# Fetching the routed rows of three expert pairs by indirect transfers instead of one-hot products

## The chip, the core and the metric

One core of a Trainium2 chip runs the whole program. Its engines work side by side, each through its own list of instructions in order: PE (TensorE, matrix products and transposes), DVE (VectorE), ACT (ScalarE), POOL (GpSimd) and SP (SyncE), which here issues nearly all DMA transfers. The transfers themselves are carried by 16 DMA engines. An instruction starts when its engine is free and the semaphores that it waits for are set. The metric is the time on the device of one execution in microseconds (us), lower is better.

## The reference

Two blocks run one after the other on 512 tokens of width 1024. The change lies in the first block's expert layer, `expert_choice`. Each of the 16 experts picks its 64 best tokens (cap = 2 * 512 / 16), takes their rows, runs a gated network of width 1024 on them and adds the weighted result back:

```python
def expert_choice(h, w_router, w_gate, w_up, w_down):
    b, l, _ = h.shape
    cap = CAP_FACTOR * l // N_EXPERTS
    aff = jax.nn.softmax(jnp.einsum('bld,de->ble', h, w_router).astype(jnp.float32), axis=-1)
    vals, idx = lax.top_k(jnp.swapaxes(aff, 1, 2), cap)
    bidx = jnp.arange(b)[:, None, None]
    xs = h[bidx, idx]
    hid = jax.nn.silu(jnp.einsum('becd,edf->becf', xs, w_gate)) * jnp.einsum('becd,edf->becf', xs, w_up)
    y = jnp.einsum('becf,efd->becd', hid, w_down) * vals[..., None].astype(h.dtype)
    return jnp.zeros_like(h).at[bidx, idx].add(y)
...
        hx2 = modulate(rmsnorm(x, g_norm2[l]), sh2, sc2)
        x = x + ga2 * expert_choice(hx2, w_router[l], w_gate_e[l], w_up_e[l], w_down_e[l])
```

`rmsnorm` scales a token's row by a factor of its own, and `modulate` scales and shifts it column by column. What is fetched in the kernel is the row times its factor; the columns' scale and shift are applied after the transpose, where the columns lie on the partitions.

## The kernel before

Before the stage (`phase_a2`) the residual `xres` is finished token tile by token tile (four tiles of 128 tokens). `ev_x` adds the branch's output and sums the squares on ACT, and `row_rstd` turns the sums into the tile's factor `rs[t]`. `logits` transposes all tokens, multiplies by the router and takes the softmax. A loop of eight rounds on DVE then finds the 64 best tokens of every expert. The result is `idxF`, 128 x 8: column p holds the token numbers of pair p, 64 of expert 2p above 64 of expert 2p+1. Beside this chain PE works on a projection of the second block's memory (`mem_k`, `mem_v`, lines 89 to 91 on the tiles `wH`, `wL`, `mH`, `mL`).

The stage itself (`phase_b`) runs over eight pairs of experts. For one pair:

- `gather(p)` brings the 128 rows to PE, transposed: `rows_b` spreads the pair's token numbers over the partitions with a product (tile `bcI`, L1060) and compares them with the token numbers on DVE (`G`, 4 tiles of 128 x 128, L1063). `G` is one-hot in the tokens and carries their factor. Then 8 column blocks x 4 token tiles = 32 products `xres` by `G` (L1101) give `xT`.
- `pair_mm` (L1090) multiplies by the gate and the up matrix, each 2 x 1024 x 1024. `hidden` multiplies both results and transposes them (L1128).
- `pair_mm` on the down matrix and `scatter` (L1141 to L1152): ACT and POOL split the weighted result into two parts (`yH`, L1146, and `yL`, L1147), PE puts them at their tokens' places (`mm2`, L96 and L97), and DVE adds. Pair 7 has `last_down` (L1118), whose two halves of the output come one after the other, and a tile `gg` in between.

In an instruction listing a product of 64 rows is one of two that share PE, and a listed fp32 product is two instructions in the trace.

Weights come in chunks of 1 MB, 8 for a gate, up or down matrix of a pair, 24 a pair. Each is one transfer issued by SP in the program's order (`raw`, L118) into a tile `raw` of 8 KB a partition. `raw_tile` gives the tiles in turn from four pools of 16 buffers in all: a list of pools is walked round and round, and within a pool its buffers follow one another. Asking for a tile outside this walk (`gg`, `self.rawp.tile`) moves the turn of the pool `rawp` alone. A transfer waits until what lay in its buffer was read, and SP, which issues in order, stands still meanwhile, with all transfers behind it.

A scheduler orders the instructions of each engine from the program's order and its model of durations; the listings below show the result.

## Time and profile before

| | us |
|---|---|
| median of 3 runs | 1707.64 (1706.93 to 1708.19) |
| profiled execution | 1707.27 |
| span of its trace | 1705.5 |
| PE busy | 1574.8 (92%) |
| DVE busy | 855.0 (50%) |
| ACT busy | 613.2 (36%) |
| POOL busy | 565.1 (33%) |

The first expert stage lies at about 533 to 1015 us of the span. Windows show what each engine did in such a stretch, a timeline gives single instructions in order of time, and the waits tell who stood still and for whom. A row of a timeline that covers several instructions has their number behind an x, and its length is that of all together. In brackets stands how long the engine was idle before it, and what ended that. The times of SP's rows are those of issuing a transfer, and a transfer lands later.

### The profile page before, as it was taken

Reading aid. Unit: us, or ns where it says so; the run is one execution under the profiler, and the core shown is the slowest. Engines: PE = TensorE matmul, PEld = TensorE weight load, DVE = VectorE, ACT = ScalarE, POOL = GpSimd, SP = SyncE. Lnnn points to the kernel's source line nnn. Section 1 sums busy time; section 2 is a strip of 40 time slices with the busy share of each in tenths; the row PEclk is TensorE's granted clock in tenths of the full one; section 3 lists DMA queues with packets and bytes.
Section 4 is the critical chain, followed back from the end, with each engine's and each line's share of the span. In section 5 each row is a group of like instructions: output and inputs, shape, how many; then the busy total and the mean of one; then the engine's idle time right before and its main releaser. Section 6 shows DMA issues by size and latency. Waiting matters only on the chain. (4 is left out here: it accounts for less than half of the span.)

```text
span 1705.5 us, 20869 instructions
## 1 busy us (share of the span) xinstructions
PE 1574.8 (92%) x7702; PEld 1044.6 (61%) x7702; DVE 855.0 (50%) x1595; ACT 613.2 (36%) x1277; POOL 565.1 (33%) x447
## 2 busy tenths in 40 slices
PE   5988899999999999999999979999999989789994
PEld 3766667777776444344344337778676766566663
DVE  4388554423554122022102137997754473667776
ACT  3443364433432000000000034325763354467773
POOL 1223324344523000000000014576443342657765
PEclk9989999999999999999999989999999999889997
DMA  8522413354746999999999983232112328369944
GB/s 290 187 98 89 134 56 111 129 183 155 273 163 256 397 408 409 409 409 409 409 409 408 408 266 128 88 99 75 51 49 87 124 86 322 111 244 344 343 162 166
DMA packets 165548, 381.23 MB, mean 224 GB/s; under 512 B 16302, under 2 KB 74742, under 8 KB 165436
## 3 DMA queue, kind: packets, MB, share of 16 engines
q1 hardware_dynamic: 161116, 371.63, 58.9%
q0 software_dynamic: 4320, 8.16, 1.3%
q8 instruction: 63, 1.03, 0.2%
q14 instruction: 49, 0.40, 0.1%
HBM read 367.40 MB, written 19.93 MB: 227 GB/s over the span
## 5 line engine op out<-in xcount | busy, mean ns | idle before, releaser
L130 POOL TENSOR_TENSOR wL<-raw,wH 128x512 fp32r<-128x512 f32 x220 | 312.5, 1426 | 420.7 <-ACT wH L129 394.8
L1090 PE MATMUL ps<-raw,xT 128*64 128x512 f32 x1024 | 240.8, 595 | 0.0
L129 ACT ACTIVATE wH<-raw 128x512 fp32r<-128x512 f32 x240 | 149.6, 628 | 253.1 <-PE ps L90 145.6
L1090 PEld LDWEIGHTS ps<-raw,xT 128*64 128x64 f32 x1024 | 74.3, 137 | 137.3 <-issue 133.4
L1147 POOL TENSOR_TENSOR yL<-y,yH 128x512 fp32r<-128x512 f32 x14 | 17.9, 1279 | 419.4 <-ACT yH L1146 409.2
L1144 DVE SCALAR_TENSOR_TENSOR y<-ps,valF,ga 128x512 f32<-128x512 f32 x16 | 12.0, 751 | 226.2 <-PE ps L1090 206.8
L91 PE MATMUL ps<-raw,wL 128*128 128x512 f32 (+1 forms) x320 | 120.6, 377 | 3.0 <-POOL wL L130 3.0
L89 PE MATMUL ps<-raw,wH 128*128 128x512 f32 (+1 forms) x320 | 121.4, 379 | 0.7 <-ACT raw L188 0.7
L90 PE MATMUL ps<-raw,wH 128*128 128x512 f32 (+1 forms) x320 | 121.0, 378 | 0.0
L1338 DVE SCALAR_TENSOR_TENSOR cacc<-upad,dwc,cacc 128x512 f32<-128x512 f32 x120 | 117.8, 1035 | 0.9
L1090 PE MATMUL ps<-raw,hidT 128*64 128x512 f32 x448 | 109.2, 594 | 2.9 <-DMA raw<-in_w_down_e 2.9
L89 PE MATMUL ps<-hx,wH 128*128 128x512 f32 x224 | 92.3, 412 | 2.0 <-ACT wH L129 2.0
L91 PE MATMUL ps<-hx,wL 128*128 128x512 f32 x224 | 90.1, 402 | 1.2 <-POOL wL L130 1.2
L1904 DVE TENSOR_TENSOR wL<-raw,wH 128x512 fp32r<-128x512 f32 x96 | 88.5, 976 | 4.7 <-ACT wH L1903 3.4
L1924 POOL TENSOR_TENSOR dL<-raw,dH 128x512 fp32r<-128x512 f32 x64 | 81.7, 1295 | 27.8 <-ACT dH L1923 27.3
L90 PE MATMUL ps<-hx,wH 128*128 128x512 f32 x224 | 90.8, 405 | 0.0
L1146 ACT ACTIVATE yH<-y 128x512 fp32r<-128x512 f32 x16 | 10.0, 626 | 212.4 <-DVE y L1144 212.4
L1129 ACT ACTIVATE hidT<-pa 128x512 f32<-128x512 f32 x16 | 9.6, 597 | 205.0 <-PE pa L1128 205.0
L1090 PEld LDWEIGHTS ps<-raw,hidT 128*64 128x64 f32 x448 | 36.2, 137 | 73.5 <-issue 62.9
L91 PEld LDWEIGHTS ps<-raw,wL 128*128 128x128 f32 x320 | 61.1, 191 | 15.0 <-POOL wL L130 3.4
L89 PEld LDWEIGHTS ps<-raw,wH 128*128 128x128 f32 x320 | 61.3, 192 | 12.3 <-ACT raw L188 1.1
L90 PEld LDWEIGHTS ps<-raw,wH 128*128 128x128 f32 x320 | 61.1, 191 | 11.5 <-issue 0.5
(618 smaller groups left out, 3401.6 us busy)
## 6 DMA issues: line engine op xcount, KB each, us to landing
raw<-in_w_gate_e SPq DMA_DIRECT2D x64, 1024.0 KB
raw<-in_w_up_e SPq DMA_DIRECT2D x64, 1024.0 KB
raw<-in_w_down_e SPq DMA_DIRECT2D x64, 1024.0 KB
raw<-in_w_in SPq DMA_DIRECT2D x34, 1024.0 KB
raw<-in_w_ada SPq DMA_DIRECT2D x24, 1024.0 KB
raw<-in_expert_w_gate SPq DMA_DIRECT2D x32, 512.0 KB
raw<-in_expert_w_up SPq DMA_DIRECT2D x32, 512.0 KB
raw<-in_expert_w_down SPq DMA_DIRECT2D x16, 1024.0 KB
```

Source lines behind the costliest of these rows:

```text
L89: mm(ps, l[0], r[0], start=first, stop=False)
L90: mm(ps, l[0], r[1], start=False, stop=False)
L91: mm(ps, l[1], r[0], start=False, stop=last)
L129: i = self.nc.scalar.activation(out=H, in_=raw_ap, func=AF.Copy)
L130: j = (eng or self.lsub).tensor_tensor(out=L, in0=raw_ap, in1=H, op=OP.subtract)
L1090: nc.tensor.matmul(ps[o, :], act[:, k, o], r[:, q, h * 512:(h + 1) * 512], start=k == 0, stop=k == 7, tile_position=(0, 64 * i))
L1144: V.scalar_tensor_tensor(y, py[e], self.valF[:, p:p + 1], ga2[:, e, :], op0=OP.mult, op1=OP.mult)
L1146: AC.activation(out=H, in_=y, func=AF.Copy)
L1147: (nc.gpsimd if p < 7 else V).tensor_tensor(out=L, in0=y, in1=H, op=OP.subtract)
L1338: V.scalar_tensor_tensor(acc, src, c, acc, op0=OP.mult, op1=OP.add)
L1904: V.tensor_tensor(out=L3, in0=w, in1=H3, op=OP.subtract)
L1924: (nc.gpsimd, V)[DL[i]].tensor_tensor(out=L, in0=src, in1=H, op=OP.subtract)
```

## The change

After `rs[t]` is known, ACT writes the token tile times its factor into two tiles `xn` and SP writes them to `xnd`, a table of 512 rows of 4 KB in device memory. The token numbers are also kept as integers (`idxU`). For the pairs 3, 5 and 7 `gather` no longer builds `G`: POOL issues an indirect transfer that fetches the 128 rows named by a column of `idxU` into a tile of the ring of weight buffers, and PE transposes them in 8 blocks. The other five pairs are gathered as before. `idxF` and `valF` move to another pool.

```diff
--- before.py
+++ after.py
@@ -31,6 +31,7 @@
 NRAW_B2 = 3
 NRAW_B3 = 6
 NRAW_B4 = 1
+ROWS_D = 3, 5, 7
 NRAW_D = 4
 NGA = 24
 NY = 3
@@ -887,6 +888,7 @@
             V.tensor_tensor(sel, sel, ident[:, q:q + 16], op=OP.add)
         nc.sync.dma_start(out=wr, in_=I["w_router"][0].rearrange("(k p) c -> p k c", p=128))
         self.rs4 = cst.tile([128, 4], F32, name="rs4")
+        self.xnd = self.drp.tile([512, 1024], F32, name="xnd")
         self.tokid = cst.tile([128, 4], F32, name="tokid")
         nc.sync.dma_start(out=self.tokid, in_=I["tokid"])
         affT = self.pa(256, name="affT")
@@ -987,6 +989,11 @@
                 self.mm3(ps, (mS2[0][k][:, tk], mS2[1][k][:, tk]), wS[k], k == 0, k == 7)
             ev_x(t, 1, ps)
             rs[t] = self.row_rstd(sm, sss[t], out=self.rs4[:, t:t + 1])
+            for e in range(2):
+                c = slice(e * 512, (e + 1) * 512)
+                xn = tc_(name="xn")
+                AC.activation(out=xn, in_=xres[:, t, c], func=AF.Copy, scale=rs[t])
+                nc.sync.dma_start(out=self.xnd[tk, c], in_=xn)
         logits()
         late.close()
         rows = self.pool(right, "rows", 1, "right")
@@ -1030,11 +1037,13 @@
         V.tensor_tensor(bidx, two[:, 1, 0:16], two[:, 3, 0:16], op=OP.subtract)
         V.tensor_tensor(bidx, bidx, low, op=OP.mult)
         V.tensor_tensor(bidx, bidx, two[:, 3, 0:16], op=OP.add)
-        self.idxF = cst.tile([128, 8], F32, name="idxF")
-        self.valF = cst.tile([128, 8], F32, name="valF")
+        self.idxF = rows.tile([128, 8], F32, name="idxF")
+        self.idxU = rows.tile([128, 8], U32, name="idxU")
+        self.valF = rows.tile([128, 8], F32, name="valF")
         for par in range(2):
             o = slice(par * 64, par * 64 + 64)
             V.tensor_copy(self.idxF[o, :], bidx.rearrange("c (p two) -> c p two", two=2)[:, :, par])
+            V.tensor_copy(self.idxU[o, :], self.idxF[o, :])
             V.tensor_copy(self.valF[o, :], best.rearrange("c (p two) -> c p two", two=2)[:, :, par])
         mem_k()
         G0 = self.rows_b(0)
@@ -1091,12 +1100,22 @@
             return pss
 
         def gather(p):
-            G = G0 if p == 0 else self.rows_b(p)
+
             xT = xp.tile([128, 8, 128], F32, tag="xT", name="xT")
+            if p in ROWS_D:
+                x = self.raw_tile(1, 1024)[:, 0, :]
+                nc.gpsimd.indirect_dma_start(out=x, out_offset=None, in_=self.xnd[:, :],
+                                             in_offset=bass.IndirectOffsetOnAxis(ap=self.idxU[:, p:p + 1], axis=0),
+                                             bounds_check=511, oob_is_err=False)
+            else:
+                G = G0 if p == 0 else self.rows_b(p)
             for e in range(2):
                 ps = self.pa()
                 for q in range(4):
                     k = 4 * e + q
+                    if p in ROWS_D:
+                        nc.tensor.transpose(ps[:, q * 128:(q + 1) * 128], x[:, k * 128:(k + 1) * 128], ident)
+                        continue
                     for t in range(4):
                         nc.tensor.matmul(ps[:, q * 128:(q + 1) * 128], xres[:, t, k * 128:(k + 1) * 128], G[:, t, :], start=t == 0, stop=t == 3)
                 self.scale_T(xT[:, 4 * e:4 * e + 4, :].rearrange("p k s -> p (k s)"), ps, self.gs2, self.sh2, 4 * e)
```

The listings that follow give instructions of an engine in its order, after the scheduler; line numbers of the changed kernel are higher than those before (L1090 becomes L1099, L118 becomes L119).

PE of the kernel before, from the last row of a middle pair's scatter to the next pair's down products; `bcI` and `G` are the tiles of `rows_b`, `xT` the gathered rows, `hid` the hidden layer:

```order
L97 MATMUL pa<-yL,PT 128x512
L1060 MATMUL bcI<-ident,idxF 128x128
L1090 MATMUL ps<-raw,xT 64x512 x6
L1101 MATMUL pa<-G,xres 128x128 x32
L1090 MATMUL ps<-raw,xT 64x512 x25
L1128 MATMUL pa<-ident,hid 128x128 x4
L1090 MATMUL ps<-raw,xT 64x512
L1128 MATMUL pa<-ident,hid 128x128 x4
L1090 MATMUL ps<-raw,xT 64x512 x31
L1090 MATMUL ps<-raw,hidT 64x512 x32
```

PE of the kernel after, in the pair that gathers rows for pair 3:

```order
L98 MATMUL pa<-yL,PT 128x512
L1117 MATMUL pa<-ident,raw 128x128 x4
L1099 MATMUL ps<-raw,xT 64x512 x2
L1117 MATMUL pa<-ident,raw 128x128 x4
L1099 MATMUL ps<-raw,xT 64x512 x29
L1147 MATMUL pa<-ident,hid 128x128 x8
L1099 MATMUL ps<-raw,xT 64x512 x32
L1099 MATMUL ps<-raw,hidT 64x512 x32
```

The product for `bcI` and the 32 products of L1101 are replaced by two groups of four transposes (L1117) directly behind the scatter; the products on the weights around them are the same in number.

SP of the kernel before, the last pair's eight down chunks with the semaphores that each waits for. DMAHW0 to 7 are the completion counters of SP's transfers, which take turns; PE is the counter of PE's reads. A `raw` tile's number names the tile that the program asked for:

```order
L118 DMA raw_6608<-in_w_down_e 128x4x512 [waits DMAHW5_49,PE_49]
L118 DMA raw_6630<-in_w_down_e 128x4x512 [waits DMAHW6_49,PE_49]
L118 DMA raw_6606<-in_w_down_e 128x4x512 [waits DMAHW7_49]
L118 DMA raw_6618<-in_w_down_e 128x4x512 [waits DMAHW0_49]
L118 DMA raw_6632<-in_w_down_e 128x4x512 [waits DMAHW1_49,PE_49]
L118 DMA raw_6620<-in_w_down_e 128x4x512 [waits DMAHW7_49,DMAHW2_49,PE_49]
L118 DMA raw_6642<-in_w_down_e 128x4x512 [waits DMAHW3_49]
L118 DMA raw_6644<-in_w_down_e 128x4x512 [waits DMAHW4_49]
```

SP of the kernel after, from the sixth up chunk of the last pair to the last down chunk:

```order
L119 DMA raw_6489<-in_w_up_e 128x2x1024 [waits DMAHW2_49,PE_49]
L119 DMA raw_6499<-in_w_up_e 128x2x1024 [waits DMAHW3_49,PE_49]
L119 DMA raw_6501<-in_w_up_e 128x2x1024 [waits DMAHW4_49,PE_49]
L119 DMA raw_6555<-in_w_down_e 128x4x512 [waits DMAHW5_49,PE_49]
L119 DMA raw_6565<-in_w_down_e 128x4x512 [waits DMAHW6_49,PE_49]
L119 DMA raw_6553<-in_w_down_e 128x4x512 [waits DMAHW7_49,DMAHW2_49,PE_49]
L119 DMA raw_6567<-in_w_down_e 128x4x512 [waits DMAHW0_49]
L119 DMA raw_6577<-in_w_down_e 128x4x512 [waits DMAHW1_49]
L119 DMA raw_6579<-in_w_down_e 128x4x512
L119 DMA raw_6589<-in_w_down_e 128x4x512 [waits DMAHW3_49]
L119 DMA raw_6591<-in_w_down_e 128x4x512 [waits DMAHW4_49]
```

Before, the wait for an earlier transfer's counter besides the chunk's own and for PE stands at the sixth down chunk (`raw_6620`, for the third). After, it stands at the third (`raw_6553`, for the sixth up chunk `raw_6489`), and the sixth has no wait.

ACT of the kernel before, where the tokens' squares end and the logits begin; `xo` is the squares' tile, `xT` a transposed token tile:

```order
L901 ACTIVATE xo,ss_3746<-xres 128x512
L901 ACTIVATE xo,ss_3747<-xres 128x512
L901 ACTIVATE xo,ss_3748<-xres 128x512
L942 ACTIVATE xT<-pa 128x512 x2
L901 ACTIVATE xo,ss_3749<-xres 128x512
L942 ACTIVATE xT<-pa 128x512 x2
L129 ACTIVATE wH<-raw 128x512 x2
```

ACT of the kernel after at the same place; `xn` is the tile that goes to `xnd`:

```order
L995 ACTIVATE xn<-xres,rs_3740 128x512 x2
L903 ACTIVATE xo,ss_3748<-xres 128x512
L995 ACTIVATE xn<-xres,rs_3740 128x512 x2
L903 ACTIVATE xo,ss_3749<-xres 128x512
L995 ACTIVATE xn<-xres,rs_3740 128x512 x2
L903 ACTIVATE xo,ss_3750<-xres 128x512
L995 ACTIVATE xn<-xres,rs_3740 128x512 x2
L944 ACTIVATE xT<-pa 128x512 x2
L130 ACTIVATE wH<-raw 128x512 x2
L944 ACTIVATE xT<-pa 128x512 x2
L130 ACTIVATE wH<-raw 128x512
```

The eight copies to `xn` stand between the squares, and all four copies to `xT` come behind the last of them.

## Rows read from the trace of the kernel before

**Rows 1.** Windows; per engine busy us (x instructions), PEclk, DMA share, GB/s

```profile
526.00:534.00 8.00, 7.81 (x39) 6.64 (x40) 1.90 (x6) 2.93 (x5) 3.91 (x3) 1.00 0.08 28
...
540.00:545.00 5.00, 5.00 (x28) 2.02 (x28) 1.37 (x4) 0.00 (x0) 0.00 (x0) 1.00 0.05 18
...
568.00:980.00 412.00, 402.15 (x1932) 171.75 (x1930) 81.72 (x163) 23.99 (x42) 17.91 (x14) 1.00 1.03 409
```

**Rows 2.** Timeline of POOL, 560 to 1010 us: start, length, operation, idle time before

```profile
607.67 1.29 POOL L1147 TENSOR_TENSOR yL<-y,yH 128x512 fp32r<-128x512 f32 x1 [76.16 <-ACT yH L1146]
...
665.12 1.28 POOL L1147 TENSOR_TENSOR yL<-y,yH 128x512 fp32r<-128x512 f32 x1 [53.24 <-ACT yH L1146]
...
723.27 1.28 POOL L1147 TENSOR_TENSOR yL<-y,yH 128x512 fp32r<-128x512 f32 x1 [54.18 <-ACT yH L1146]
...
903.43 1.28 POOL L1147 TENSOR_TENSOR yL<-y,yH 128x512 fp32r<-128x512 f32 x1 [57.44 <-ACT yH L1146]
...
964.82 1.28 POOL L1147 TENSOR_TENSOR yL<-y,yH 128x512 fp32r<-128x512 f32 x1 [57.41 <-ACT yH L1146]
```

**Rows 3.** Timeline of SP's queue, late in the stage: start, length of eight issues

```profile
862.41 20.39 SPq L118 DMA_DIRECT2D raw<-in_w_down_e  x8
...
944.29 20.42 SPq L118 DMA_DIRECT2D raw<-in_w_up_e  x8
```

**Rows 4.** Groups of PE instructions, shapes apart, 480 to 1040 us

```profile
L1090 PE MATMUL ps<-raw,hidT 128*64 128x512 f32 x448 | 109.2, 594 | 2.9 <-DMA raw<-in_w_down_e 2.9
...
L1101 PE MATMUL pa<-G,xres 128*128 128x128 f32 x512 | 59.2, 276 | 0.0
...
L1128 PE MATMUL pa<-ident,hid 128*128 128x128 f32 x64 | 10.5, 286 | 0.2 <-DVE hid L1125 0.2
...
L1060 PE MATMUL bcI<-ident,idxF 128*128 128x128 f32 x16 | 3.2, 284 | 0.3 <-DVE idxF L1037 0.3
```

**Rows 5.** The tile xsb (second expert stage), whole trace: durations and landing

```profile
L1872 POOL DMA_INDIRECT xsb<-hmd,trow x16: 990/1372/1405, 1496.6 to 1625.2; - x16
...
DMA to landing us min/median/max: 4.3/8.3/9.4
```

**Rows 6.** Windows at the end of the stage

```profile
980.00:990.00 10.00, 9.79 (x62) 6.00 (x60) 1.37 (x2) 2.99 (x6) 0.00 (x0) 0.99 1.04 385
...
990.00:994.00 4.00, 4.00 (x12) 1.17 (x14) 0.00 (x0) 0.59 (x1) 0.00 (x0) 0.60 0.60 224
...
994.00:996.00 2.00, 2.00 (x12) 0.73 (x10) 0.00 (x0) 0.00 (x0) 0.00 (x0) 1.00 0.00 0
...
996.00:1004.00 8.00, 7.16 (x32) 2.20 (x29) 0.00 (x0) 0.00 (x0) 0.00 (x0) 1.00 0.97 349
```

**Rows 7.** Timeline of SP's queue, the last eight chunks

```profile
964.80 31.88 SPq L118 DMA_DIRECT2D raw<-in_w_down_e  x8
```

**Rows 8.** Waits of SP's queue, 964 to 1012 us: total, times, longest

```profile
SPq L118 <- PE ps L1118: 13.1, 3, 6.4
```

**Rows 9.** Timelines of POOL, ACT and PE at the start of the stage

```profile
501.75 0.55 POOL L235 TENSOR_TENSOR rs<-rv,mhalf 128x1 f32<-128x1 f32 x1 [5.61 <-DVE rv L231]
...
504.48 0.60 ACT L942 ACTIVATE xT<-pa 128x512 f32<-128x512 f32 x1 [1.27 <-DVE xT L944]
...
524.01 0.27 PE L1022 MATMUL pst<-ident,vi 128*64 128x128 f32 x1 [2.16 <-DVE vi L1020]
...
526.40 0.48 PE L89 MATMUL ps<-wH,mH 128*128 128x512 f32 x1
...
533.09 0.39 PE L91 MATMUL ps<-wH,mL 128*128 128x512 f32 x1
```

**Rows 10.** Timelines of PE and ACT at the end of the stage

```profile
1000.31 3.79 PE L1118 MATMUL ps<-raw,hidT 128*64 128x512 f32 x16 [0.84 <-DMA raw<-in_w_down_e]
...
1005.53 1.21 PE L96 MATMUL pa<-yH,PT 128*128 128x512 f32 x4 [1.43 <-ACT yH L1146]
...
1018.89 0.61 ACT L1248 ACTIVATE nsq<-xg 128x512 f32<-128x512 f32 x1
```

## The prediction, made before the changed kernel ran

> **What bounds the kernel now.** I read the stretches first. From 568 to 980 us, which is nearly the whole first expert stage, the DMA engines are full: share 1.03, 409 GB/s [rows 1]. PE is busy 402 of these 412 us, so it is nearly full too, and the question is which of the two sets the pace. The POOL operation that closes a pair's down projection gives the period of a pair [rows 2]: 57.45 and 58.15 us between the first three rows, 61.39 between the last two (964.82 - 903.43). The queue's rows explain the second number [rows 3]: eight 1 MB weight chunks take 20.4 us, 2.55 us a chunk, and a pair has 24 of them, so 24 x 2.55 = 61.2 us. The early pairs run faster than the transfers only because PE begins with full buffers behind (the queue had stopped: 28 GB/s at 526 to 534 us, 18 at 540 to 545 [rows 1]). After that PE waits for data in small pieces: in the whole stage 2.9 us on `raw<-in_w_down_e` [rows 4]. So the stage is bound by its 192 MB of weights, and PE has about 3 us a pair to spare (61.4 - 58.2).
>
> **PE work taken out.** A gather by one-hot products costs 59.2/8 = 7.4 us of PE for 64 instructions, and its broadcast 3.2/8 = 0.4 us [rows 4]. The eight transposes that replace it are the operation of L1128, 10.5 us for 64, so 1.3 us [rows 4]. Three pairs: 3 x (7.4 + 0.4 - 1.3) = 19.5 us of PE work less, and 3 x 4 DVE operations. If PE set the pace this would be the gain. It does not: what hides it is the transfer period of 61.2 us, and PE's need in a pair already fits in 57.5 to 58.2. I count the 19.5 us at zero; if that cover is gone it is a rival (below). The one-hot pairs 1, 2, 4, 6 stay as they are.
>
> **Bytes added (+3.85 us).** Each fetch brings 128 rows of 4 KB, 0.524 MB, into a weight buffer. Three are 1.57 MB, and at 409 GB/s [rows 1] that is 3.85 us of the full DMA engines, in the stretch that has none to spare. From below: if the second kind of transfer fits into gaps of the first, nothing; from above: the trace's only indirect transfers, in the second expert stage, land 4.3 to 9.4 us after issue and occupy POOL 1.37 us [rows 5]; three of the shortest would be 12.9 us if all other traffic stood still for them, which rows without two streams cannot exclude. I take 3.85, because rows 1 and 3 show the engines full and not the issue; only a third way to share them, one transfer at a time, gives the upper end. The writes of the normalised rows (512 x 1024, 2.1 MB, 5.1 us at 409) fall where the rate is 28 and 18 GB/s or just ahead of it, so they cost nothing unless they delay the first weight chunks, which stand buffered.
>
> The Trainium skill, "DMA: Bandwidth & Descriptors", section "Issuing engines are not separate DMA queues", says that transfers issued from different engines end on the same 16 DMA engines, so that issuing from another engine adds no bandwidth. No row of this trace shows POOL and SP transfers together in a full stretch. By that rule the term stands at +3.85; without it the sum below would be 3.85 lower.
>
> **The wait for a fetched row (0).** POOL issues the fetches for pairs 3, 5 and 7 behind the subtractions of pairs 0, 2 and 4. The transposes stand behind the scatter of pairs 1, 3 and 5, one period of about 58 us later [rows 2]. In between a fetch waits for its buffer, whose last reader stands about half a period ahead of the transposes on PE; so some 25 us are left, an estimate from the order and the period, and a landing takes at most 9.4 [rows 5]. Behind the fetch on POOL stands the subtraction of the next pair, which comes only just ahead of those transposes. Cost 0; if a fetch were issued no sooner than its rows are needed, a landing of 9.4 less the 3 us to spare, 6.4 a pair.
>
> **The ring of weight buffers moves (-4.4 us).** This is the part that the diff does not say. A fetch takes a turn in the ring, so every later chunk lands in another buffer, and what a chunk waits for changes. Before, the last eight down chunks show a hole [rows 6]: 385 GB/s from 980, 224 from 990, 0 from 994 to 996, 349 from 996. In order, the sixth of them has to wait until PE has read the third. The queue's row says the same: eight issues take 31.9 us in place of 20.4 [rows 7], and it waited three times for PE at L1118, 6.4 us the longest [rows 8]. The hole is worth 4 x (385 - 224)/385 = 1.67, plus 2, plus 8 x (385 - 349)/385 = 0.75: 4.4 us of transfer. After the change that sixth chunk waits for nothing, and the wait is at the third of the eight, for the sixth up chunk. That one lands and is read while four further chunks, 10.2 us, are queued, so the queue should not run dry. I take -4.4; bounds 0 (the hole moves) and -6.4 (the longest wait).
>
> **The start of the stage (-0.7 us).** ScalarE now makes eight copies of 128x512 among the router's copies. A copy of that shape is 0.60 us [rows 9]. The two of the last token tile wait for its factor, POOL 501.75 + 0.55 = 502.30, and stand ahead of the four logit copies, the last of which began at 504.48. Two copies ahead of them push the logits by about 1.35 us. Top-k follows them, and PE waited 2.16 us for it at 524.01. But nine matrix products of the memory projection, 9 x (533.09 - 526.40)/29 = 2.1 us, move from behind that wait to ahead of the logits. PE's wait becomes 2.16 + 1.35 - 2.1 = 1.4, so the first gather starts 0.75 us earlier; I take -0.7. Bounds: -2.1 if the logits do not move, +1.4 if they slip by 3.5 us (all copies in line). An earlier start counts in full only because transfers begin again when PE frees buffers.
>
> **The end of the stage (-1 us).** The last half's products and its scatter are in a different order after the change: 17 products of the last half run, then scatter rows and products alternate. PE waited 0.84 us for the last chunks and 1.43 us for `yH` [rows 10]. With the chunks there earlier the first goes, and products fill part of the second. Against it ScalarE now runs all eight squares of the first half (0.61 us each) before the second half's `yH`, which could hold that up by three of them, 1.8 us; the squares left afterwards are fewer by as many. Net -1, bounds -3 and +1.8.
>
> **Sum.** +3.85 - 4.4 - 0.7 - 1.0 = -2.25. The profiled execution took 1707.27, of which 1705.5 is the span; 1707.27 - 2.25 = 1705.0. The median of the three runs, 1707.64, stands 0.37 above it, so on that scale 1705.3. I give 1705.2.
>
> **Rivals.** 0.2% of this kernel, 3.4 us, is about what a measurement can tell from no change.
> 1. The hole only moves. The third chunk's wait stops the queue earlier instead of the sixth's. Then +3.85 - 0.7 = +3.2, and with 5 us more for five chunks that stand behind the wait up to +8: 1710.5 to 1715. For it: the wait is there in the order of the changed kernel. Against it: it is for a chunk read long before. It decides from the point where PE reads the sixth up chunk more than 10.2 us after it landed.
> 2. The clock falls. PE's free time grows from 3 to 9.5 us in pairs 3, 5 and 7, all of it waits for data. In the trace the granted clock is 1.00 (2.4 GHz) through 568 to 980 and 0.60 at 990 to 994 [rows 1, 6], a stretch that is partly at 1.2 GHz, so the lower level is in reach. From 990 to 1004 PE is busy 4.00 + 2.00 + 7.16 = 13.2 us [rows 6]; ten of them at half speed, where most ran at full speed before, would cost 5: 1705.0 + 5 = 1710. Against it: waits shorter than a chunk, since every chunk of 2.55 us still brings its products.
> 3. The full gain. If PE sets the pace, 19.5 us go: 1707.6 - 19.5 - 1.7 = 1686.4. Against it: the periods of rows 2 and 3.
> 4. Start and end both give their bounds: +3.85 - 4.4 - 2.1 - 3 = -5.7, about 1701.5.
> 5. The change does not do what it says: if the fetched rows come late, PE stands and the weight buffers stay full; 6.4 us a pair would be 19 in all, 1724. Against it: the 25 us above.
>
> The Trainium skill, "TensorE: Matmul & The Clock Gate", section "HAM oscillation — how this bites in real kernels", describes kernels in which PE waits for data between bursts and the clock drops for the work that follows. That is rival 2; this trace does not bear it out so far, since it shows 1.00 in a stretch in which PE waited 2.9 us for the down weights.
>
> **Chances.** Forecast 0.62, with its own range 1701.5 to 1708.5 (the bounds of start and end, and bytes half hidden). Rival 1 0.12, rival 2 0.12, rival 3 0.03, rival 4 0.08, rival 5 0.03. The range for 8 in 10 is 1699.5 to 1711.5: it takes in the forecast, rivals 2 and 4, and the lower edge of rival 1. The upper end of the bytes' bound, 12.9, is left to the part outside it. Faster by over 3.4 us means below 1704.2: about four tenths of the forecast's cases (0.26), rivals 3 and 4: 0.37. Slower, above 1711.1: rival 1, rival 5, a third of rival 2: 0.19. Within: 0.44.
>
> **What would show it.** Right: the period of the last pairs is 61.4 us, plus 1.3 in the pairs in which a fetch lands; 0 GB/s appears nowhere between 980 and 1004; the first gather starts within 1 us of 532.6; the product rows of pairs 3, 5, 7 wait more on weight chunks, 6 us a pair. Wrong: a period under 60 us in the last pairs (then PE set it); a row in which L1117 waits for `raw<-xnd`; a granted clock below 0.9 between 600 and 980.

## The result: slower by 0.55%

The changed kernel takes 1717.63 us (median of 6 runs, 1714.98 to 1718.74), the kernel before 1707.97 (6 runs). The ratio is 1.0055, 95% interval 1.0045 to 1.0065, so about 9.4 us slower (the medians differ by 9.7), above the range that was given. The profiled execution took 1717.18 us, its span is 1714.8: 9.3 more than before.

The windows of the changed kernel (columns as in [rows 1]) answer to [rows 1] and [rows 6]:

```profile
568.00:980.00 412.00, 394.37 (x1740) 156.78 (x1738) 77.35 (x151) 24.00 (x42) 21.14 (x17) 1.00 1.03 409
980.00:990.00 10.00, 9.89 (x46) 3.40 (x42) 1.33 (x2) 0.07 (x1) 0.00 (x0) 1.00 1.02 386
990.00:994.00 4.00, 3.89 (x31) 3.73 (x32) 0.05 (x1) 2.65 (x5) 0.00 (x0) 0.94 1.05 391
994.00:996.00 2.00, 2.00 (x9) 1.32 (x9) 0.00 (x0) 0.86 (x2) 0.00 (x0) 0.50 1.05 386
996.00:1004.00 8.00, 8.00 (x30) 2.45 (x28) 0.00 (x0) 0.00 (x0) 0.00 (x0) 0.73 1.05 386
```

The transfers still fill the stage at 409 GB/s, PE's busy time there falls from 402.15 to 394.37, and the hole at 994 to 996 is gone: 386 GB/s where there was 0. But in the last three stretches the granted clock is 0.94, 0.50 and 0.73 where it was 0.60, 1.00 and 1.00. PE spends more of the end of the stage at the low level of 1.2 GHz.

The groups of PE instructions (480 to 1040 us) answer to [rows 4] for the work taken out:

```profile
L1120 PE MATMUL pa<-G,xres 128*128 128x128 f32 x320 | 37.0, 276 | 0.0
...
L1117 PE MATMUL pa<-ident,raw 128*128 128x128 f32 x24 | 3.8, 279 | 0.0
```

The one-hot products (L1120, L1101 before) fall from 59.2 to 37.0 us and 3.8 us of transposes come in: with 1.1 us less for `bcI` that is the 19.5 us that were reckoned. PE's busy time falls by less, since the products on the weights (L1099, L1090 before) take 329.7 us instead of 318.4 in the 412 us of the first window.

The timeline of POOL (start, length, operation) answers to [rows 2] and shows a fetch:

```profile
608.53 1.29 POOL L1166 TENSOR_TENSOR yL<-y,yH 128x512 fp32r<-128x512 f32 x1 [76.20 <-ACT yH L1165]
...
719.69 1.28 POOL L1166 TENSOR_TENSOR yL<-y,yH 128x512 fp32r<-128x512 f32 x1 [49.69 <-ACT yH L1165]
...
752.54 1.02 POOL L1107 DMA_INDIRECT raw<-xnd,idxU  x1 [28.87 <-PE ps L1099]
...
907.96 1.27 POOL L1166 TENSOR_TENSOR yL<-y,yH 128x512 fp32r<-128x512 f32 x1 [28.85 <-ACT yH L1165]
...
969.37 1.28 POOL L1166 TENSOR_TENSOR yL<-y,yH 128x512 fp32r<-128x512 f32 x1 [57.43 <-ACT yH L1165]
```

The rows without a fetch close the down projections of pairs 0, 2, 5 and 6. The row at 719.69 is 3.58 us earlier than 723.27 before, since PE has no one-hot products in that pair. By 969.37 this is gone: 4.55 us later than 964.82. The period of the last pair, 61.41 us, is what it was (61.39).

The tile of the table (duration of the fetch on POOL as min/median/max, and landing) answers to [rows 5]:

```profile
L1107 POOL DMA_INDIRECT raw<-xnd,idxU x3: 1003/1022/1229, 640.7 to 878.1; - x3
...
DMA to landing us min/median/max: 7.6/7.7/8.3
```

A fetch of 1.0 to 1.2 us on POOL lands 7.6 to 8.3 us later with the transfers at 409 GB/s. The one shown is issued at 752.54 for transposes that begin at 788.17; the three are issued 31 to 36 us ahead of their use. So the rows are never late, and no row shows a wait for them.

The waits of PE in the stage (total, times, longest) answer to the wait in [rows 4]:

```profile
PE ps L1099 <- DMA raw<-in_w_down_e: 7.8, 13, 0.6
```

It was 2.9 us (five times, 0.6 at most): PE stands more, as it has less to do and the chunks come no faster. On gate chunks it waits another 1.9 us (three times, 0.6 at most), 0 before.

The rows at the start of the stage answer to [rows 9]: ACT before (one row that was not shown), ACT after, PE after:

```profile
499.21 0.60 ACT L942 ACTIVATE xT<-pa 128x512 f32<-128x512 f32 x1 [4.08 <-PE pa L940]
```

```profile
501.79 1.34 ACT L995 ACTIVATE xn<-xres,rs 128x512 f32<-128x512 f32 x2 [1.04 <-POOL rs L236]
503.03 1.06 ACT L944 ACTIVATE xT<-pa 128x512 f32<-128x512 f32 x2
...
507.93 0.60 ACT L944 ACTIVATE xT<-pa 128x512 f32<-128x512 f32 x1 [1.27 <-PE pa L942]
```

```profile
526.88 0.27 PE L1029 MATMUL pst<-ident,vi 128*64 128x128 f32 x1 [2.66 <-DVE vi L1027]
...
534.18 7.31 PE L1120 MATMUL pa<-G,xres 128*128 128x128 f32 x64
```

The copies to `xn` are L995, those of the logits L944 (L942 before). The first logit copy begins at 503.03 instead of 499.21, the last at 507.93 instead of 504.48, PE waits 2.66 us for top-k (2.16 before), and the first gather begins at 534.18 (533.32 before, by [rows 9]: the last product of the projection at 533.09).

The end of the stage on PE, before (two rows that were not shown) and after, answers to [rows 10]:

```profile
986.12 3.83 PE L1170 MATMUL pa<-rows,ident 16*128 16x128 f32 x32
989.89 9.59 PE L1118 MATMUL ps<-raw,hidT 128*64 128x512 f32 x34
```

```profile
990.69 4.63 PE L1189 MATMUL pa<-rows,ident 16*128 16x128 f32 x32
995.25 10.46 PE L1137 MATMUL ps<-raw,hidT 128*64 128x512 f32 x34
...
1013.48 3.65 PE L1137 MATMUL ps<-raw,hidT 128*64 128x512 f32 x14
1018.83 1.20 PE L97 MATMUL pa<-yH,PT 128*128 128x512 f32 x4 [1.70 <-ACT yH L1165]
```

L1170, now L1189, is the block of 32 small products that fills `gg`; L1118, now L1137, are the last down products. Before, 32 and 34 instructions took 3.83 and 9.59 us, now 4.63 and 10.46, with no wait for a chunk inside: the same instructions with more of their time at the lower clock. The granted clock fell at 989.82 before, 0.13 us ahead of the end of the block, and rose at 993.24; after the change it fell at 993.54, with 1.78 us of the block still to come, and rose at 1000.37.

At the very end, POOL's closing instruction, before and after, in the answer on the line that closes the program (its duration in ns three times, then its first and last start):

```profile
L2072 POOLq INC_SWDGE_SEM  x1: 772/772/772, 1701.3 to 1701.3; - x1
```

```profile
L2091 POOLq INC_SWDGE_SEM  x1: 832/832/832, 1710.4 to 1710.4; - x1
```

The program's last DVE operation ends at 1699.30 before and 1706.34 after, 7.04 later. POOL's closing instruction comes 9.1 us later, the end of the span 9.3. Where the list of POOL stands still in between is told under e9.

### The profile page after: what moved, and what is told of

The parts are those of the page before. It is cut to its first block, busy times and chain, and to the rows that moved or that the text cites. A ratio compares the mean times of both kernels' runs of the same rounds, so it can differ in the third digit from the quotient of the medians.

```text
span 1714.8 us, 20572 instructions
## 1 busy us (share of the span) xinstructions
PE 1575.3 (92%) x7528; PEld 1031.2 (60%) x7528; DVE 850.3 (50%) x1585; ACT 618.7 (36%) x1285; POOL 566.6 (33%) x450
## 5 line engine op out<-in xcount | busy, mean ns | idle before, releaser
L1099 PE MATMUL ps<-raw,xT 128*64 128x512 f32 x1024 | 244.6, 596 | 2.1 <-DMA raw<-in_w_gate_e 1.9
L1099 PEld LDWEIGHTS ps<-raw,xT 128*64 128x64 f32 x1024 | 77.2, 137 | 143.8 <-issue 133.9
L1099 PE MATMUL ps<-raw,hidT 128*64 128x512 f32 x448 | 119.7, 598 | 7.9 <-DMA raw<-in_w_down_e 7.8
L1099 PEld LDWEIGHTS ps<-raw,hidT 128*64 128x64 f32 x448 | 39.2, 136 | 85.2 <-issue 59.9
```

The source lines that it names most:

```text
L1099: nc.tensor.matmul(ps[o, :], act[:, k, o], r[:, q, h * 512:(h + 1) * 512], start=k == 0, stop=k == 7, tile_position=(0, 64 * i))
```

## The experiments

Every profile can be cut at the same six places: the last token factor on POOL (`rs`, 501.75 before), the first one-hot product on PE (533.32), the first subtraction of pair 6 on POOL (964.82), the first transpose of `hn` on PE, the tile with which the second block begins (1021.17), the end of the last DVE operation (1699.30) and the end of the span (1705.5; spans are given to 0.1 us, and the last piece is no finer). The table gives how much longer each of the five pieces between them is than in the kernel before, in us of the one profiled execution, and in the column "low" what the last pair loses to the lower clock: the sum over windows of 1 us, from 984 to 1006, of 1 minus the granted clock (1.71 before). "Time" is the difference of the medians, each against the kernel before of its own comparison, and the interval that of the ratio.

| run | start | bytes | end of stage | low | rest | close | time | ratio |
|---|---|---|---|---|---|---|---|---|
| changed kernel | +1.40 | +3.69 | +1.92 | 3.41 | +0.57 | +2.26 | +9.7 | 1.0045 to 1.0065 |
| e12 changed, again | +1.44 | +3.76 | +1.91 | 3.41 | +0.23 | +2.10 | +7.8 | 1.0029 to 1.0057 |
| e13 before, again | -0.01 | -0.04 | +0.12 | 1.71 | +1.09 | +0.03 | -0.8 | 0.9984 to 1.0002 |
| e1 table only | +1.41 | -0.09 | +1.71 | 3.41 | +1.51 | 0.00 | +3.1 | 1.0009 to 1.0027 |
| e2 ring only | +0.01 | +0.12 | +0.23 | 1.70 | -0.36 | +0.07 | -0.6 | 0.9989 to 1.0008 |
| e3 fetched, unused | +1.41 | +3.64 | +1.88 | 3.41 | +0.52 | +2.25 | +8.1 | 1.0033 to 1.0061 |
| e4 no table | +0.06 | +3.78 | +1.94 | 3.42 | +4.10 | +0.46 | +8.5 | 1.0040 to 1.0068 |
| e5 before, gg moved | +1.09 | +0.09 | -4.01 | 0.00 | +1.18 | +0.01 | -5.0 | 0.9961 to 0.9980 |
| e6 changed, gg moved | +1.42 | +3.70 | -3.32 | 0.00 | +3.76 | +1.50 | +4.4 | 1.0013 to 1.0033 |
| e7 seven pairs | +1.40 | +8.94 | -0.01 | 1.70 | +7.32 | +0.53 | +10.6 | 1.0046 to 1.0074 |
| e8 quarter rows | +1.43 | +1.15 | +1.86 | 3.41 | +1.87 | +2.09 | +4.4 | 1.0016 to 1.0035 |
| e10 before, padded | +0.05 | +0.10 | +0.05 | 1.71 | +1.01 | +0.37 | +0.1 | 0.9991 to 1.0009 |
| e11 as e5, tile kept | 0.00 | -0.17 | -3.72 | 0.00 | +0.64 | +1.23 | -2.3 | 0.9981 to 1.0000 |
| e9 changed, padded | +1.41 | +2.56 | +0.26 | 1.71 | -0.07 | +0.02 | +3.0 | 1.0009 to 1.0027 |
| e14 padded, again | +1.41 | +2.51 | +0.23 | 1.71 | -0.28 | +0.18 | +3.0 | 1.0002 to 1.0021 |

What lies ahead of the stage, where all kernels have the same work, differed by -2.1 to +2.2 us from profile to profile and is left out. "Rest", the second block, scatters too: it is +1.09 in the kernel before itself. The first three columns repeat to 0.1 us. The profile of e7 was the slowest of its runs (1725.74, median 1719.69), so its rest says little.

**e1: the table, no fetch.**

```diff
-ROWS_D = 3, 5, 7
+ROWS_D = ()
```

> The changed kernel with all eight gathers by one-hot products: the table of normalised rows is still written (eight ACT copies, eight transfers) and the numbers are kept as integers, nothing is fetched. Theory A (the +9.7 us is a sum: start +0.9 from the copies in the router's chain, bytes +3.7, tail of the last pair +1.9, the rest behind the stage): only the start is left, +0.9 us against before, and the hole in the transfers of the last pair is back, as before. Rival B (the writes or the longer chain cost more, and carry most of the loss): +4 us or more. Rival C (the copies are hidden): 0.

Measured +3.1 us. The start costs 1.41, the bytes nothing. The end of the stage has the old order and the hole, and still loses 1.71, with 3.41 in the column "low" against 1.71: exactly the clock. Two of its windows show the hole beside the low clock (third column from the right):

```profile
994.00:996.00 2.00, 2.00 (x6) 0.47 (x4) 0.00 (x0) 0.00 (x0) 0.00 (x0) 0.50 0.48 178
996.00:998.00 2.00, 2.00 (x8) 0.71 (x6) 0.00 (x0) 0.00 (x0) 0.00 (x0) 0.50 0.00 0
```

Theory A was too small by that (and by 0.5 in the start), rival C falls, and B's 4 us are not reached.

**e2: the ring's turns alone.**

```diff
+            if p in ROWS_D:
+                nc.gpsimd.memset(self.raw_tile(1, 1024)[:, 0, 0:8], 0.0)
             xT = xp.tile([128, 8, 128], F32, tag="xT", name="xT")
```

> The kernel before, with one turn of the weight ring taken in the gathers of pairs 3, 5 and 7 (a tile of which POOL clears 8 columns, never read), nothing else: so the last pair's chunks lie in the same buffers as in the changed kernel. My prediction on record: the hole goes and the end is 1 us shorter, -5.4 us. Theory A (PE, not the transfers, sets the end of the last pair, the hole cost PE only its wait of 0.84 us, and the new order of products and scatter costs more): +1 to +2.5 us. Rival D (the ring's shift makes no difference to the time, and the tail's loss comes from the fetches): 0.

Measured no difference. The windows show the hole gone, as forecast, with the clock back at 1.00 by 994:

```profile
990.00:994.00 4.00, 4.00 (x16) 1.17 (x14) 0.00 (x0) 0.09 (x1) 0.00 (x0) 0.69 1.04 386
994.00:996.00 2.00, 2.00 (x12) 0.66 (x10) 0.00 (x0) 0.00 (x0) 0.00 (x0) 1.00 1.05 388
```

The end of the stage is 0.23 us longer than before, not 5.4 shorter. This decides the ring term: filling the hole gave nothing, where PE's wait for the last chunks, 0.84 us in [rows 10], was the most that it could give. That the new order of products and scatter takes the 0.84 back is argued, not shown by itself. Theory A's +1 to +2.5 is too much. Rival D has the time right; its other half, that the tail's loss comes from the fetches, falls with e1, which has the loss and no fetch.

**e3 and e4: the fetch without its use, and without the table.**

```diff
-            else:
-                G = G0 if p == 0 else self.rows_b(p)
+            G = G0 if p == 0 else self.rows_b(p)
...
-                    if p in ROWS_D:
-                        nc.tensor.transpose(ps[:, q * 128:(q + 1) * 128], x[:, k * 128:(k + 1) * 128], ident)
-                        continue
```

> The changed kernel with the three fetches, whose rows nobody reads; all eight gathers are one-hot products. So the 19.5 us of PE work are not saved. Theory A (transfers set the pace, the saving is worth nothing): within 1.5 us of the changed kernel, +8 to +11 against before. Rival E (PE sets the pace in part of the stage, and the saving gave something back): slower than the changed kernel by 4 to 19 us.

```diff
-            for e in range(2):
-                c = slice(e * 512, (e + 1) * 512)
-                xn = tc_(name="xn")
-                AC.activation(out=xn, in_=xres[:, t, c], func=AF.Copy, scale=rs[t])
-                nc.sync.dma_start(out=self.xnd[tk, c], in_=xn)
...
-                nc.gpsimd.indirect_dma_start(out=x, out_offset=None, in_=self.xnd[:, :],
+                nc.gpsimd.indirect_dma_start(out=x, out_offset=None, in_=I["x"][0],
```

> The changed kernel without the table: the eight copies and the eight transfers to it are gone, and the fetches take rows of the program's input x of the same shape (so the three pairs work on other rows; the values are not the reference's). Theory A: the start's +0.9 goes, the rest stays: +8 to +9 against before. Rival B: the loss is mostly the table's, so +4 or less.

In e3 the 19.5 us of PE work are back, and the stage is not longer: bytes +3.64 against +3.69. So that work was worth nothing, and rival E falls. The first subtraction of pair 6 stands at 969.87 in e3 and at 969.37 in the changed kernel. In e4 the start is back to +0.06, which puts the whole +1.4 on the table; the run does not separate its copies from its transfers, but ACT's rows above show the copies in the way. Bytes and end stay, as theory A said, and rival B falls. That e4's time, +8.5, lies where theory A put it is luck in part: the close is 1.8 us shorter than in the changed kernel, and the rest 3.5 us longer. In e4 other rows are worked on, so its rest cannot be compared.

**e5 and e6: the small products taken out.**

```diff
-        rows2 = xp.tile([16, 128], F32, tag="rows2", name="rows2", bufs=1)
...
-                    for q in range(4):
-                        r = 4 * i + q
-                        nc.tensor.matmul(ps[:, q * 128:(q + 1) * 128], ident[0:16, r:r + 1].to_broadcast([16, 128]), rows2, start=True, stop=True)
-                    AC.activation(out=gg[:, i // 2, (i % 2) * 512:(i % 2 + 1) * 512], in_=ps, func=AF.Copy)
...
+                py = last_down(hT)
+                gg = self.gg = self.rawp.tile([128, 2, 1024], F32, tag="raw", name="raw")
+                for i, n in enumerate((I["g_final"], I["norm_mix_g_2"][0])):
+                    nc.sync.dma_start(out=gg[:, i, :], in_=n.rearrange("(o c) -> o c", o=1).to_broadcast([128, 1024]))
```

> The kernel before, with the tile gg (two gain vectors spread over the partitions) brought by two broadcast transfers behind the last down chunk, in place of 32 small products on PE ahead of the last down products. Theory A (PE sets the end of the last pair; the block costs its 3.83 us and leaves PE at 1.2 GHz for 4.0 us behind it, which costs 2.0): the granted clock stays at 1.00 through the last pair and the time falls by 5 to 6 us. Rival F (the clock falls there whatever PE did before): clock low again, -3 to -4 us. Rival G (the transfers set the end of the last pair): -1 to +2.5 us, since 1 MB more is moved.

> The changed kernel with the same replacement of gg. Theory A (in the changed kernel the low clock lasts 7.0 us instead of 4.0, 1.5 us of its tail's loss): block 4.63 and 3.5 for the clock go, -7 to -8 us against the changed kernel, that is +1 to +2.5 against before, and against the run of the same edit on before it stands at +6.5 to +8. Rival F: -4 to -5 against the changed kernel. Rival G: -1 to +2.5 against the changed kernel.

The windows of e5 (the granted clock is the third column from the right):

```profile
990.00:994.00 4.00, 2.89 (x13) 0.91 (x13) 0.00 (x0) 0.00 (x0) 0.00 (x0) 1.00 1.05 386
994.00:996.00 2.00, 1.15 (x6) 0.27 (x3) 0.75 (x1) 0.09 (x1) 0.00 (x0) 1.00 1.04 386
996.00:1004.00 8.00, 7.40 (x34) 3.16 (x36) 3.17 (x5) 0.54 (x1) 0.35 (x1) 1.00 1.04 387
```

The clock stays at 1.00 through the last pair in both, so rival F falls: it is the block of small products that the low clock follows. Rival G falls too. Both gain about 5 us (e6: 4.4 against 9.7), less than theory A said in e6: at the end of the stage 4.0 and 5.2 us, where 3.83 us of block and the column "low" make 5.5 and 7.2. PE waits more there. Its waits for the last chunks and in the scatter add up to 5.0 us in e5 against 3.8 before, and to 4.9 in e6 against 2.4 in the changed kernel; two of e5's:

```profile
991.37 3.78 PE L1115 MATMUL ps<-raw,hidT 128*64 128x512 f32 x16 [1.11 <-DMA raw<-in_w_down_e]
...
1009.54 1.20 PE L97 MATMUL pa<-yL,PT 128*128 128x512 f32 x4 [0.98 <-DVE yL L1144]
```

e5 is faster than both kernels. A variant of it, e11, that leaves the two vectors' small tile and its transfers where they were:

> The kernel before with gg brought by two broadcast transfers behind the last down chunk, as in the run of that edit before, but with the small tile of the two vectors and its two transfers left in at the start of the stage, where without them the first gather had begun 1.1 us later behind the last token factor. Theory A: the end as in that run, 5 us below before, and the start back, so 5 to 6.5 us below before. Rival: the start was chance, -5 us again.

It has the start back (0.00) and the end of the stage at -3.72, but only 2.3 us in the time. Two kernels that differ in a small tile and its two transfers gave -5.0 and -2.3 us; the profiles agree on 3.7 to 4.0 us at the end of the stage. Theory A of e11 put the time 5 to 6.5 below, so it missed. 1.2 of the 2.7 us between the two lie in the close of e11 (+1.23; POOL's closing instruction is on time there, SP's last waits end 1.2 us later), against 1.1 that its start is shorter; the rest the runs do not resolve.

**e7 and e8: more bytes, fewer bytes.**

```diff
-ROWS_D = 3, 5, 7
+ROWS_D = 1, 2, 3, 4, 5, 6, 7
```

> The changed kernel with the rows of seven pairs (1 to 7) fetched, 3.67 MB instead of 1.57. Theory A (each fetch costs its bytes at 409 GB/s, 1.28 us, and the PE work saved nothing): last subtraction on POOL of pair 6 at +0.9 + 8.6 = 9.5 us behind the kernel before, the whole +13 to +15. Rival E (PE sets the pace while the buffers are full, so more PE work saved gives something back): less than the changed kernel's +9.

```diff
-                x = self.raw_tile(1, 1024)[:, 0, :]
-                nc.gpsimd.indirect_dma_start(out=x, out_offset=None, in_=self.xnd[:, :],
+                x = self.raw_tile(1, 256)[:, 0, :]
+                nc.gpsimd.indirect_dma_start(out=x, out_offset=None, in_=self.xnd.rearrange("t (q c) -> (t q) c", q=4),
...
-                                             bounds_check=511, oob_is_err=False)
-            else:
-                G = G0 if p == 0 else self.rows_b(p)
+                                             bounds_check=2047, oob_is_err=False)
+            G = G0 if p == 0 else self.rows_b(p)
...
-                    if p in ROWS_D:
-                        nc.tensor.transpose(ps[:, q * 128:(q + 1) * 128], x[:, k * 128:(k + 1) * 128], ident)
-                        continue
```

> The changed kernel with three fetches of 128 rows of 1 KB (a quarter of the bytes, the same number of rows), which nobody reads; all gathers are one-hot products. Theory A (bytes): the fetches cost 0.96 us instead of 3.7, so the whole is 2.5 to 3 us below the same kernel with 4 KB rows (+8.1 against before), near +5.4. Rival H (the cost is per row or per transfer, not per byte): +8 as with 4 KB.

The bytes term is +8.94 for seven fetches (8.98 worked out at 409 GB/s), +3.69 for three (3.85) and +1.15 for the bytes of three quarters of a fetch (0.96). So it goes by bytes, and rival H falls; e8's time, +4.4, is 1 us below theory A's +5.4. The first subtraction of pair 0 stands 6.09 us earlier in e7 than before, that of pair 6 10.56 later: seven gathers saved 45 us of PE, and the transfers took all of it back. The whole, +10.6, missed both of e7's expectations, theory A's +13 to +15 and rival E's less than +9: theory A had left 3.5 to 5.5 us for what comes behind the stage's bytes, and of the changed kernel's 4.2 in end and close e7 pays 0.5.

**e9, e10, e12, e13, e14: what belongs to the kernel.** Two terms had no cause yet, the close and the longer low clock.

```diff
             hid = silu(pg)
+            if p == 1:
+                pad = xp.tile([16, 8], F32, tag="pad", name="pad", bufs=1)
+                for _ in range(16):
+                    nc.gpsimd.memset(pad, 0.0)
```

> The changed kernel with 16 clears of a 16x8 tile more on POOL in the first expert stage, where POOL is idle. In the changed kernel 8.5 us lie between the last DVE operation and the end of the span, 6.2 in the kernel before and in four of the experiments; POOL's last instruction comes 2.1 us late there. Theory I (it depends on where POOL's list of instructions happens to end, which the three fetches shift): with 16 more instructions the stretch is 6.2 to 6.7 again, and the time 1 to 2 us below the changed kernel's. Rival J (it comes with the fetches themselves): 8.5 again, no change against the changed kernel.

> The kernel before with the same 16 clears on POOL. Theory I: the stretch behind the last DVE operation can become longer, up to 8.5 us, without any fetch; the rest of the time is unchanged (0 to +2 us). Rival J: 6.2 us, no change.

> The changed kernel unchanged, on the same chip as the next two. Open is 6 us between it and the kernel with 16 clears more on POOL, measured on different chips: 2.2 lie behind the last DVE operation, about 1.9 in a shorter stretch at 1.2 GHz in the last pair (7.0 against 3.3 us), about 1 in the rate of the transfers. Theory K (the length of the low clock and the rate of transfers differ from execution to execution and chip to chip, only the 2.2 belong to the kernel): the stretch at 1.2 GHz may come out at 3 to 4 us this time, the end at 8.5 again, the time +6 to +9.5 against before. Rival L (all of it belongs to the kernel): 7.0 and 8.5 us again, +9 to +10.

> The kernel before unchanged, with a profile on the same chip. Theory K: the low clock in the last pair between 3 and 7 us, not necessarily 4.0; the end 6.2. Rival L: 4.0 and 6.2 again.

> The changed kernel with 16 clears more on POOL, again, on the chip of the two above. Theory K: the end 6.2 again, so 1.5 to 3 us below the changed kernel; the low clock between 3 and 7 us. Rival L: the end 6.2, the low clock 3.3, 5 to 6 us below the changed kernel.

Sixteen clears on POOL that nobody reads make the changed kernel about 5 us faster (e12 and e14 on one chip: 1716.76 and 1711.97), where theory I said 1 to 2. The close is 6.2 us again (6.4 in e14) instead of 8.5, as theory I said; with the same clears the kernel before, e10, has 6.6 us and keeps its time, ratio 0.9991 to 1.0009. POOL's closing instruction and the last DVE operation of e9:

```profile
L2095 POOLq INC_SWDGE_SEM  x1: 831/831/831, 1704.7 to 1704.7; - x1
```

```profile
1701.57 1.41 DVE L2043 SCALAR_TENSOR_TENSOR raw<-xres,rr,raw 128x512 f32<-128x512 f32 x2 [0.66 <-POOL rr L236]
```

POOL's closing instruction follows the last DVE operation by 1.7 us here, by 4.1 in the changed kernel and by 2.0 before. So the close does not come with the fetches, which are in the padded kernel and in e4 (+0.46) too; it changes with the length of POOL's list of instructions. The traces show how. Counted with its waits and register operations, POOL's list has 785 instructions before, 805 in the changed kernel (e12 too), 804 in e3 and e8, 803 in e6, 801 in e4 and e10 and 821 in the padded kernel. In all seven profiles with 801 to 805, POOL stands still between its 795th instruction and the next: for 1.9 and 2.35 us with 805, 2.1 and 2.3 with 804, 1.4 with 803, 0.4 with 801. With 805 that place is among the last waits ahead of the closing instruction:

```profile
L2091 POOLq EVENT_SEMAPHORE  x5: 17/43/43, 1707.7 to 1710.3; - x5
```

These five stand within 0.3 us in the kernel before (1700.9 to 1701.2). A list of 795 or fewer ends before that place. In the lists of 820 and 821 it lies some 20 us ahead of the last DVE operation, among vector instructions of 1.3 to 1.8 us, and no pause is seen there. So the place is fixed in the list, with fetches or without (e10 has none), and it costs time where the closing part of the list lies on it. What makes POOL pause there no run isolates. e11's close, with 784, is SP's and not this.

The low clock is 3.41 in both executions of the changed kernel and 1.71 in both of the kernel before and of the padded one, so it goes with the program and not with the chip (rival L; theory K falls for it), and in every row of the table where it is 3.41 the end of the stage costs 1.7 to 1.9, where it is 1.7 at most 0.3. Windows of 2 us of e14, where the changed kernel has 0.50 from 994 to 1000:

```profile
994.00:996.00 2.00, 2.00 (x13) 1.24 (x13) 0.00 (x0) 1.19 (x2) 0.00 (x0) 0.73 1.04 383
996.00:998.00 2.00, 2.00 (x8) 0.70 (x6) 0.00 (x0) 0.00 (x0) 0.00 (x0) 0.50 1.08 391
998.00:1000.00 2.00, 2.00 (x10) 0.57 (x9) 0.00 (x0) 0.00 (x0) 0.00 (x0) 0.92 1.03 388
```

Neither table nor fetches set the one or the other length: the table is in all kernels with 3.41 but e4, the fetches in all but e1, and e7, e9 and e14 have both and 1.7. It goes with where the clock falls in the block of small products. In the six profiles with 3.41 the block still ran for 0.95 to 3.9 us after the fall, in the seven with 1.7 for 0.5 us at most, or it had just ended. Why the fall comes sooner or later in the block stays open.

That the padded kernel pays 2.5 us for its bytes instead of 3.7, twice, is the rate of its transfers. Between the two cuts of that column e14 moves the same 175.5 MB as the changed kernel. From 20 us behind the first gather to the second cut the mean rate is 409.0 GB/s in e9 and e14, where the changed kernel has 407.9 and e12 407.8. A difference of 0.3% is 1.2 us over this stretch, a third of the bytes term. What raises the rate stays open.

## Why the prediction was wrong, step by step

**PE work taken out, 0: right.** e3 puts the work back and loses nothing. Rival 3, PE setting the pace, was rightly small.

**Bytes, +3.85: right,** 3.69, and in proportion to the bytes over a factor of nine (but 2.5 in the padded kernel, whose transfers ran 0.3% faster). The upper bound of 12.9 and the lower of 0 are both excluded. The rule of the Trainium skill in "DMA: Bandwidth & Descriptors", section "Issuing engines are not separate DMA queues", holds here with that number: POOL's fetches took their time out of SP's stream, +3.69 us for 1.57 MB.

**The wait for a fetched row, 0: right.** Issued 31 to 36 us ahead of the use, landed after 7.6 to 8.3.

**The ring, -4.4: wrong, and the step that failed by most.** The hole did go, as the order said. But I priced it in the time of the queue, and the queue was not what ended last there. From the first subtraction of pair 6 on, PE has neither a gather nor a gate product left, and its chunks lie ready; [rows 10] held the answer, one wait of 0.84 us for the last chunks. What the hole could give was 0.84, which the step on the end counts once more, and e2 measured 0.2 the other way.

**The start, -0.7: wrong in sign,** +1.40. The part on PE was right (2.1 us of products moved ahead). Top-k slipped by 3.4 us against the token factor, not by 1.35: before, ACT made the first of its four logit copies at 499.21, ahead of the last factor; now none begins before 503.03, behind all of `xn`. The order showed that, and I moved the logits only by the two copies of the last tile. The upper bound, +1.4, is what was measured.

**The end, -1: wrong,** +1.92, of which 1.70 is the clock. Rival 2 had the clock as cause, but from waits for data; those grew (7.8 us in the stage on `raw<-in_w_down_e`, 2.9 in [rows 4]) and the clock stayed at 1.00 through them. It fell in the last part of the small products, with PE busy throughout, as it had in the kernel before, and e5 and e6, without them, keep 1.00. The rule of the Trainium skill in "TensorE: Matmul & The Clock Gate", section "HAM oscillation — how this bites in real kernels", in which waits for data bring the clock down, does not explain this fall: no such wait in the stage was longer than 0.6 us, and none was followed by a lower clock. Behind the stage the trace agrees with it: in the kernel before the clock falls again at 1017.13, inside PE's longest wait there, 6.05 us for `hn`:

```profile
1017.00:1020.00 3.00, 0.00 (x0) 0.00 (x0) 2.34 (x8) 2.87 (x8) 1.70 (x7) 0.52 0.50 57
```

```profile
1021.17 1.97 PE L1262 MATMUL pa<-ident,hn 128*128 128x128 f32 x8 [6.05 <-DVE hn L1259]
```

**Missing:** the close, +2.26, which no step had. It hangs on the length of POOL's list, which the change made 20 instructions longer (785 to 805; e1, without the fetches, has 788 and pays nothing).

With the sizes measured, 1.40 + 3.69 + 1.92 + 2.26 is 9.3, the span's difference; what lies ahead of the stage (-0.54) and the second block (+0.57) cancel. Against the forecast of -2.25 the ring is off by 4.6 us, the end by 2.7, the close by 2.3 and the start by 2.1 (the end's +1.92 taken as 0.2 of the ring and 1.7 of the clock), while the bytes came out 0.2 lower. Of the prediction's own signs, none of the "wrong" ones came, the last period and the filled hole came as said, and the first gather (534.18) and PE's waits (7.8 and 1.9 us in all, where 6 a pair were said) did not: the signs watched the stage, and much of the loss lies at its edges.

## What to carry to other kernels

Ask of a stretch which of the two, the engine or the queue, ended last in it before pricing a hole in the queue: a hole is worth no more than the wait that its consumer shows. Work taken off an engine that outruns the transfers buys nothing, and bytes added to a full stretch cost their size over its rate, whoever issues them. A small block of thin products in front of dense ones can cost more than its own time: here 3.8 us in the block, and 1.7 or 3.4 us more by the lower clock that comes with it.

## What the runs showed of the hardware

- A block of 32 small products over 16 partitions, 3.8 us with PE busy, went with a fall to 1.2 GHz in all 13 profiles that had it, from 3.9 us ahead of its end to 0.25 us behind it, for 3.4 or 6.8 us (twice the 1.7 or 3.4 of the column); in the three that did not have it the clock stayed up until 1009.9 at least. Which property of the block does it no run isolates.
- An indirect fetch of 128 rows of 4 KB kept POOL for 1.0 to 1.2 us and landed after 7.6 to 8.3 us with the transfers at 409 GB/s (changed kernel).
- Chunks in runs of 2 KB moved at 386 to 391 GB/s (the last pair's down chunks, windows of the changed kernel), those in runs of 4 KB at 409.
- Sixteen small clears on POOL, in time in which it was idle, made the stretch behind the last DVE operation of the changed kernel 2 us shorter (8.5 to 6.2 and 6.4). In seven profiles POOL paused at the same place of its list, behind its 795th instruction, for 0.4 to 2.35 us.
